# Half-array side tiles made whole, and the order of a chunked recurrence rebuilt, in a four-layer streaming encoder

## The chip, the cores and the metric

The kernel runs on one core of one Trainium2 chip. The metric is device time in microseconds (us). Before the change three runs gave a median of 2739.07 us (2736.65 to 2741.68). Engines are named as in the profile: PE (TensorE matmul), PEld (its weight load), DVE (VectorE), ACT (ScalarE), POOL (GpSimd), SP (SyncE, which issues the DMAs).

## The reference, cut to what matters

320 columns are processed at once: 256 frames of a prompt and 64 frames of a running stream ("sample") that has a cache of 512 frames. The model width is 2048. Every layer is `x + W_out(mixer(rmsnorm(x)) * silu(gate))`, and the mixers of the four layers are A, B, C, A:

```python
# A: differential attention, 16 heads of 2x64
p = attn_map(q1, k1) - lam * attn_map(q2, k2);  o = p @ v_all
o = o * rsqrt(mean(o * o) + 1e-5) * subln_g
# B: sparse attention, 16 heads of 128 on 4 key heads; an indexer picks the top keys
# C: RWKV-7, 32 heads with a 64x64 state, a scan over frames
sa = st @ (-kk_t)
st = st * w_t + outer(sa, kk_t * a_t) + outer(v_t, k_t)
o_t = st @ r_t
# then a group norm of o per head, a bonus term, and the gate
```

## The kernel before

**The main stream.** Every projection is a chain of 128-row weight tiles (`MTile`). A weight tile is loaded, split on ACT and DVE into a high and a low part in a `ring`, and multiplied in 16 k-steps of three fp32r matmuls of 320 columns; these are the rows with `ring` in their input. A `Group` of one tile runs its 16 k-steps in turn; a group of several tiles is "outer": for each quarter of the k-steps it goes through all its tiles, so it holds one PSUM bank for each tile from its start. `start_group` must have all of a group's banks before its first matmul. Banks 0 and 1 are kept for accumulators; banks 2 to 7 are shared with the side work, and an outer group may take any that is free.

**The side work.** Attention, norms, and the recurrence are Python generators (tasks of a `Stage`). A program-time planner (`Model`, `Sched.pump`) puts their instructions between the k-steps of the main stream. It gives out an operation of a task when its model says that the inputs are ready; for PE it adds `SLACK`, 400 ns, so that the main stream isn't held up. The order is fixed in the program; at run time each engine works its queue in order.

**Layer A** (twice, 16 heads each). `sample(h)` computes the sample's scores for both maps on 128 rows (64 frames of map 1, then of map 2), takes each map's exponential into its own 64-row buffer (`PS`), joins them with lambda, and transposes the joined map with five transposes whose input has 64 rows. `attend(h)` does the same for the prompt and then all of the head's value products: six matmul records on the whole array, and ten for the sample that write 64 rows each (four matmuls of `cv`, the two halves of the array in turn, and one of `vt` with 64 input rows). An fp32 matmul leaves two records, a transpose one. The end of the head transposes the output `ot` in three pieces, the third with 64 input rows.

**Layer B**: the sample's value product of each pair of heads ends in a matmul with 64 input rows; there are eight pairs.

**Layer C** runs stages v, then k and r, then g. In the k stage `on_k` (16 times) has a three-piece group of sums and a three-piece transpose, each with a 64-row third piece; `finish_rstd` (five times in the kernel) is built alike. `batch(n)` inverts 32x32 blocks of the recurrence in 31 steps of a multiply and a subtract, on POOL for the first two batches and on DVE for the last. The g stage (stage `sg`) runs 16 gate tiles, and beside them 16 chains, one for a pair of heads: `load_chain` takes a set of buffers (`SETS`: three at first, a fourth and a fifth later) and issues five loads; `corners` finishes the inverse with two bursts of small matmuls; `steps` walks over chunks 0 to 3 of the prompt, with three bursts of PE work for each chunk (products into `scr`, through ACT; products with `yv`, through ACT; the new state and the output), and a second task walks over the sample's chunk 4 with three more. Then `chain` loads the bonus (`bv_d`), norms and gates the output, transposes it in three pieces, marks the operand `opo` of the output projection, and gives its set back. The scratch bank of `corners`, the bank of `steps` and that of the last transpose are taken and given back apart.

**After layer C** the output projection begins with an outer group of four tiles; its first quarter needs the results of chains 0 to 3 only, its last quarter those of chains 12 to 15. **The end** of the kernel (`ending`) multiplies 16 result tiles by the norm, four pieces on DVE and two on POOL, and stores each.

Of the kernel before, what the change touches and what calls it, by code (L numbers as in the profile page):

```python
# [16 lines left out]
D = 2048  # L17
KT = 16
# [10 lines left out]
NEG = -1.0e30  # L29

# [73 lines left out]
class Model:  # L104
# [39 lines left out]
    def cost(self, op):  # L144
# [21 lines left out]
        if op.eng == "G":  # L166
# [8 lines left out]
            return 2.3 * n + 149  # L175
# [43 lines left out]
class Sched:  # L219
# [45 lines left out]
    def pump(self):  # L265

        while True:
            self.moved, nxt = False, None
            for t in list(self.tasks):
                while self.settle(t):  # L270
# [3 lines left out]
                    r = max(self.model.ready(op) + (SLACK if op.eng == "PE" else 0.0) for op in t.queue[:n])  # L274
# [111 lines left out]
class Stage:  # L386
    def __init__(self, prev):
        self.prev = prev
        self.active = 0
        self.closed = False  # L390
# [58 lines left out]
def hybrid_kernel(ctx: ExitStack, tc: tile.TileContext, a, o, layers=DEPTH):  # L449
# [71 lines left out]
    def transposes(dst, src, n=128):  # L521

        idn = ident[0:n, 0:n]
        PE.transpose(dst[:, 0:n], src[:, 0:128], idn)
        PE.transpose(dst[:, n:2 * n], src[:, 128:256], idn)
        PE.transpose(dst[0:64, 2 * n:3 * n], src[:, 256:320], idn)

    def copy_tokens(dst, src, n=128):
        S.copy(dst[:, 0:2 * n], src[:, 0:2 * n])
        S.copy(dst[0:64, 2 * n:3 * n], src[0:64, 2 * n:3 * n])  # L530
# [119 lines left out]
    def finish_rstd(li, sq):  # L650
# [3 lines left out]
        for b in range(3):  # L654
            n = 128 if b < 2 else 64
            for i, x in enumerate((ssum, sq)):
                PE.matmul(bk.ap[0:n, b:b + 1], lhsT=x[:, b * 128:b * 128 + n], rhs=ones[:, 0:1],
                          start=i == 0, stop=i == 1)
        G.memset(sm.ap[:, 0:3], 1.0)
        V.tensor_scalar(sm.ap[:, 0:2], bk.ap[:, 0:2], 1.0 / D, 1e-6, op0=OP.mult, op1=OP.add)  # L660
        V.tensor_scalar(sm.ap[0:64, 2:3], bk.ap[0:64, 2:3], 1.0 / D, 1e-6, op0=OP.mult, op1=OP.add)
# [5 lines left out]
        for b in range(3):  # L667
            n = 128 if b < 2 else 64
            PE.transpose(bk.ap[:, b * 128:b * 128 + n], rtok[0:n, b:b + 1].to_broadcast([n, 128]), ident[0:n, 0:n])
# [5 lines left out]
    def out_groups(li, opo, prev):  # L675
# [47 lines left out]
        return ([Group(mts[0:4], on_start=lambda: spawn(st, prefetch()))] + [Group([x]) for x in mts[4:]]  # L723
                + [close], st)

    def ending(sq, yall):
        yield from finish_rstd(layers, sq)
        yield from wait(*[("y", i) for i in range(KT)])
        for n, (k0, k1, E) in enumerate(((0, 3, V), (12, 14, G), (3, 6, V), (6, 9, V), (14, 16, G), (9, 12, V))):
            t = yall[:, k0:k1]  # L730
            E.tensor_mul(t, t, rstd.unsqueeze(1).to_broadcast([128, k1 - k0, T]))
# [8 lines left out]
    def layer_a(j, li, opn, opo, prev):  # L740
# [13 lines left out]
        PS = lay.slots(4, 576)  # L754
        PT = lay.slots(2, 384)
        PTS = lay.slots(2, T)
# [35 lines left out]
        def prep():  # L792
# [4 lines left out]
            for p in PP.free:  # L797
                G.memset(p[0:64, 64:128], 0.0)
                G.memset(p[0:64, 320:384], 0.0)
            if li:  # L800
# [94 lines left out]
        def sample(h):  # L895
# [31 lines left out]
            yield  # L927

            V.reciprocal(s[0:64, 4:6], s[0:64, 2:4])
            V.scalar_tensor_tensor(s[0:64, 6:7], s[0:64, 2:3], lam[0:64], s[0:64, 5:6], op0=OP.mult, op1=OP.mult)  # L930
            V.scalar_tensor_tensor(p1.ap[0:64], p2.ap[0:64], s[0:64, 6:7], p1.ap[0:64], op0=OP.mult, op1=OP.add)
            p2.rel()
            bk = yield from banks.one()
            for i in range(4):
                PE.transpose(bk.ap[:, i * 64:(i + 1) * 64], p1.ap[0:64, 64 + i * 128:192 + i * 128],
                             ident[0:64, 0:64])
            PE.transpose(bk.ap[0:64, 256:320], p1.ap[0:64, 0:64], ident[0:64, 0:64])
            p1.rel()
# [1471 lines left out]
```

## Time and profile before

| | |
|---|---|
| runs before, median of 3 | 2739.07 us |
| the profiled execution's own time | 2740.95 us |
| its span, first to last instruction | 2739.1 us |
| PE busy | 2677.7 us |
| DVE busy | 1926.6 us |
| ACT busy | 1466.7 us |
| POOL busy | 437.3 us |
| mean granted TensorE clock | 0.990 |

The span is the time from the first to the last instruction of the profiled execution; what lies outside it is the difference to its own time. Busy times are sums for each engine; engines overlap.

### The profile page before, as it was taken

The page shows a single profiled execution, that of the slowest core. Times are in us where ns is not written, and L with a number is a line of the kernel's source. Part 1 is how long each engine was busy: PE and PEld are TensorE (multiplying, and loading weights), DVE is VectorE, ACT ScalarE, POOL GpSimd, SP SyncE. Part 2 cuts the span into 40 slices and gives each one's busy share as a digit, 9 for nine tenths or more (in the row PEclk, how much of TensorE's full clock was granted, in tenths as well). Part 3 has the DMA queues.
Part 4 walks back from the last instruction along what each step waited for, and adds up shares of the span by engine and source line. Part 5 has one row for each costly group of instructions (what it writes and reads, how often), then busy time and mean ns, then how long its engine had stood idle before and what let it go on. Part 6 is the DMA issues. An engine that isn't in the chain of part 4 may idle for free.

```text
span 2739.1 us, 53165 instructions
## 1 busy us (share of the span) xinstructions
PE 2677.7 (98%) x19594; PEld 2569.3 (94%) x19594; DVE 1926.6 (70%) x4080; ACT 1466.7 (54%) x3582; POOL 437.3 (16%) x809
## 2 busy tenths in 40 slices
PE   8999999999999999989999999999899999999997
PEld 7999999999999999989999998888799999999997
DVE  7777777765898766459766767766657777777654
ACT  5666656554444444436644453566544666666553
POOL 2000000011000000122012745365310000000011
PEclk9999999999999999989999999999999999999998
DMA  6444444455334333665667676766464444444452
GB/s 227 149 152 155 153 149 149 145 180 178 133 130 150 122 134 135 201 173 173 224 181 207 184 201 176 243 222 205 129 199 165 151 154 154 153 145 153 133 176 105
DMA packets 219979, 455.23 MB, mean 166 GB/s; under 512 B 83270, under 2 KB 149254, under 8 KB 185798
## 3 DMA queue, kind: packets, MB, share of 16 engines
q1 hardware_dynamic: 219718, 451.83, 50.6%
q8 instruction: 154, 2.52, 0.4%
q14 instruction: 107, 0.88, 0.1%
HBM read 394.20 MB, written 57.55 MB: 165 GB/s over the span
## 4 chain that ended last, share of the span: by engine, by line
PE 51%; DVE 2%; DMA 1%; issue 1%; SPq 0%; POOL 0%; ACT 0%; DVEq 0%; POOLq 0%; ACTq 0%
PE psum L209 51%; DVE arena L209 1%; SPq L209 0%; DMA rec_d<-arena 0%; DVE ring L209 0%; DMA arena<-l_d 0%; DMA raw<-in_c_w_rkvg_dram 0%; DVE op_b L209 0%; POOL arena L209 0%; ACT ring L209 0%; POOL smt L209 0%; DVEq L2406 0%; DVE op_a L209 0%; ACT arena L209 0%; DVE smt L209 0%
## 5 line engine op out<-in xcount | busy, mean ns | idle before, releaser
L209 PE MATMUL psum<-op_a,ring 128*128 128x320 f32 x8496 | 1332.4, 314 | 22.4 <-ACT op_a L209 12.4
L209 PEld LDWEIGHTS psum<-op_a,ring 128*128 128x128 f32 x8496 | 1260.2, 189 | 38.8 <-ACT op_a L209 14.5
L209 ACT CAST ring<-raw 128x512 fp32r<-128x512 f32 (+2 forms) x1228 | 754.0, 618 | 846.8 <-PE psum L209 789.1
L209 DVE TENSOR_TENSOR ring<-raw,ring 128x512 fp32r<-128x512 f32 (+2 forms) x1228 | 852.2, 699 | 443.1 <-ACT ring L209 425.9
L209 PE MATMUL psum<-op_b,ring 128*128 128x320 f32 (+1 forms) x6240 | 990.9, 314 | 5.3 <-ACT ring L209 5.3
L209 PEld LDWEIGHTS psum<-op_b,ring 128*128 128x128 f32 (+1 forms) x6240 | 921.7, 188 | 21.2 <-ACT ring L209 5.6
L209 DVE TENSOR_TENSOR arena<-psum,arena 32x320 f32<-32x320 f32 (+3 forms) x567 | 269.9, 476 | 79.8 <-PE psum L209 60.1
L209 PE MATMUL psum<-arena 128*64 128x64 f32 (+9 forms) x3428 | 297.8, 253 | 3.3 <-DVE arena L209 2.2
L209 PEld LDWEIGHTS psum<-arena 128*64 128x64 f32 (+4 forms) x3428 | 238.7, 147 | 51.4 <-issue 23.0
L209 ACT COPY arena<-psum 128x256 f32<-128x256 f32 (+9 forms) x473 | 145.2, 331 | 95.4 <-PE psum L209 82.1
L209 ACT ACTIVATE arena<-psum,smt 64x128 f32<-64x128 f32 (+5 forms) x384 | 169.6, 442 | 25.5 <-DVE smt L209 15.8
L209 POOL TENSOR_TENSOR smt<-smt,mhalf 128x3 f32<-128x3 f32 (+1 forms) x64 | 74.9, 1170 | 476.2 <-DVE smt L209 466.2
L209 POOL TENSOR_TENSOR arena<-arena 128x64 f32<-128x64 f32 (+18 forms) x218 | 135.3, 624 | 38.8 <-DMA arena<-l_d 9.7
L209 PE MATMUL psum<-cst,arena 128*128 128x128 f32 (+3 forms) x807 | 130.5, 266 | 7.6 <-DVE arena L209 6.0
L209 PEld LDWEIGHTS psum<-cst,arena 128*128 128x128 f32 (+3 forms) x807 | 92.3, 134 | 30.6 <-issue 18.6
L209 POOL MEMSET smt<- 128x3 f32 (+2 forms) x85 | 8.4, 100 | 703.9 <-DVE smt L209 703.9
L209 ACT ACTIVATE arena<-arena 128x320 f32<-128x320 f32 (+1 forms) x192 | 89.1, 472 | 42.9 <-DVE arena L209 28.8
L209 POOL TENSOR_TENSOR ssum<-ssum,arena 128x320 f32<-128x320 f32 x70 | 64.3, 919 | 298.4 <-ACT arena L209 295.1
L209 ACT CAST op_b<-arena 128x320 fp32r<-128x320 f32 (+4 forms) x198 | 78.8, 416 | 53.4 <-DVE arena L209 30.0
L209 DVE TENSOR_TENSOR arena<-arena 64x320 f32<-64x320 f32 (+13 forms) x243 | 100.0, 420 | 3.4 <-DMA arena<-l_d 0.6
L209 ACT CAST op_a<-arena 128x320 fp32r<-128x320 f32 (+2 forms) x136 | 59.9, 442 | 66.3 <-DVE arena L209 47.5
L209 DVE TENSOR_TENSOR op_b<-arena,op_b 128x320 fp32r<-128x320 f32 (+4 forms) x198 | 85.9, 455 | 1.8 <-ACT op_b L209 1.6
(95 smaller groups left out, 1370.5 us busy)
## 6 DMA issues: line engine op xcount, KB each, us to landing
raw<-in_a_w_in_dram SPq DMA_DIRECT2D x120, 1024.0 KB, 5.2
raw<-in_c_w_rkvg_dram SPq DMA_DIRECT2D x52, 1024.0 KB, 5.7
raw<-in_w_out_dram SPq DMA_DIRECT2D x48, 1024.0 KB, 5.1
raw<-in_b_w_in_dram SPq DMA_DIRECT2D x45, 1024.0 KB, 4.9
raw<-in_w_out_dram SPq DMA_DIRECT2D x64, 256.0 KB, 3.8
arena<-rec_d SPq DMA_DIRECT2D x16, 962.5 KB, 5.5
raw<-in_c_w_rkvg_dram SPq DMA_DIRECT2D x48, 256.0 KB, 4.1
out_dram<-arena SPq DMA_DIRECT2D x72, 160.0 KB, 5.1
```

The source lines that it names most:

```text
L209: return getattr(self.engines[op.eng], op.name)(*op.args, **op.kw)
```

## The change

Five groups of edits:

1. **Whole tiles.** The third piece of every three-piece group is the frames 192 to 319 instead of 256 to 319 (`BLOCKS`), so that it has 128 rows like the others. In layer A the two exponentials of the sample become one on 128 rows, five transposes of 128x128 go back into the bank of the scores, the value product becomes five matmuls of the whole array with both maps on its output rows, and lambda and the sums are applied after it. In layer B the last piece is filled up with zeros.
2. **The recurrence.** `corners`, `steps` and `chain` become one task; the sample's chunk 4 goes in step with chunk 0; one bank is held from the corners to the last transpose. The set is given back at the last step; what follows (`gated`) uses a buffer apart (`ES`, one at first, two more once the last batch is inverted). There are four sets from the start.
3. **Orders.** The slack of stage `sg` is 0. The last batch of inverses runs on POOL. `rb` in `on_k` is spread by ACT and not by POOL.
4. The output projection after layer C begins with an outer group of six tiles.
5. `ending` multiplies on DVE alone, in five pieces.

```diff
+BLOCKS = (0, 128, 192)
...
-            return 2.3 * n + 149
+            return (3.3 if 64 < op.width < 128 else 2.3) * n + 149
...
-                    r = max(self.model.ready(op) + (SLACK if op.eng == "PE" else 0.0) for op in t.queue[:n])
+                    slack = SLACK if t.stage is None else t.stage.slack
+                    r = max(self.model.ready(op) + (slack if op.eng == "PE" else 0.0) for op in t.queue[:n])
...
-        for b in range(3):
-            n = 128 if b < 2 else 64
-            PE.transpose(bk.ap[:, b * 128:b * 128 + n], rtok[0:n, b:b + 1].to_broadcast([n, 128]), ident[0:n, 0:n])
+        for b, t in enumerate(BLOCKS):
+            PE.transpose(bk.ap[:, t:t + 128], rtok[:, b:b + 1].to_broadcast([128, 128]), ident)
...
-        return ([Group(mts[0:4], on_start=lambda: spawn(st, prefetch()))] + [Group([x]) for x in mts[4:]]
+        return ([Group(mts[0:(6 if li == 2 else 4)], on_start=lambda: spawn(st, prefetch()))] + [Group([x]) for x in mts[(6 if li == 2 else 4):]]
...
-        for n, (k0, k1, E) in enumerate(((0, 3, V), (12, 14, G), (3, 6, V), (6, 9, V), (14, 16, G), (9, 12, V))):
+        for k0, k1 in ((0, 4), (4, 8), (8, 11), (11, 14), (14, 16)):
...
-            p1, p2 = yield from PS.get(2)
-            for e, p in enumerate((p1, p2)):
-                S.activation(p.ap[0:64].rearrange("p (b c) -> p b c", c=288), in_banks(sc.ap[HALF[e]]), AF.Exp,
-                             bias=s[HALF[e], 1:2], scale=0.125, accum_out=s[0:64, 2 + e:3 + e])
+            p, = yield from PS.get(1)
+            S.activation(p.ap[:, 64:640].rearrange("p (b c) -> p b c", c=288), in_banks(sc.ap), AF.Exp,
+                         bias=s[:, 1:2], scale=0.125, accum_out=s[:, 2:3])
+            yield
+            for i in range(5):
+                PE.transpose(sc.ap[:, i * 128:(i + 1) * 128], p.ap[:, i * 128:(i + 1) * 128], ident)
...
-            for i in range(4):
-                PE.matmul(ob.ap[HALF[i % 2], 256:384], lhsT=pts.ap[:, i * 64:(i + 1) * 64],
-                          rhs=cv.ap[:, i * 128:(i + 1) * 128], start=i < 2, stop=i == 3)
-            PE.matmul(ob.ap[0:64, 256:384], lhsT=pts.ap[0:64, 256:320], rhs=vt.ap[0:64, 256:384],
-                      start=False, stop=True)
+            for i in range(5):
+                PE.matmul(ob.ap[:, 256:384], lhsT=pts.ap[:, i * 128:(i + 1) * 128],
+                          rhs=cv.ap[:, i * 128 - 128:i * 128] if i else vt.ap[:, 256:384], start=i == 0, stop=i == 4)
...
-            PE.transpose(bk.ap[:, 256:320], ot.ap[0:64, 256:384], ident[0:64, 0:64])
+            PE.transpose(bk.ap[:, 256:384], ot.ap[:, 256:384], ident)
...
-            PE.matmul(ob.ap[:, 0:128], lhsT=vt.ap[0:64, 256:384], rhs=pt.ap[0:64, 512:640], start=False, stop=True)
+            PE.matmul(ob.ap[:, 0:128], lhsT=vt.ap[:, 256:384], rhs=pt.ap[:, 512:640], start=False, stop=True)
...
-        sb, sl, sg = Stage(sv), Stage(sv), Stage(sk)
+        sb, sl, sg = Stage(sv), Stage(sv), Stage(sk, 0.0)
...
-                G.tensor_copy(rb.ap.rearrange("p (b f) -> p b f", f=64),
-                              sm.ap[:, 8:14].unsqueeze(2).to_broadcast([128, 6, 64]))
+                S.copy(rb.ap.rearrange("p (b f) -> p b f", f=64),
+                       sm.ap[:, 8:14].unsqueeze(2).to_broadcast([128, 6, 64]))
...
-            E = V if n == len(batches) - 1 else G
+            E = G
...
-        SETS = Slots(sched, sets[0:3])
+        SETS = Slots(sched, sets)
+
+        late = [(lg.ap(384), lg.ap(T)) for _ in range(2)]
+        ES = Slots(sched, [(cst[:, 128:512], rstd)])
...
+        def load_bonus(p):
+            yield from wait(("late", p))
+            e = yield from ES.get()
+            Q.dma_start(e.ap[1], bv_d[p])
+            flags["es", p] = e
...
+        def chain(ps):
+
+            yield from corners(ps)
+            for p in ps:
+                spawn(sg, load_bonus(p))
+            for c in range(4):
+                now = [Step(p, c, 0) for p in ps]
+                if not c:
+                    now += [Step(p, 4, 1) for p in ps]
+                for x in now:
+                    for e in range(2):
+                        PE.matmul(x.scr[HALF[e]], lhsT=x.mv[:, 0, e, x.c], rhs=x.st[:, e, x.c, :],
+                                  start=True, stop=True)
+                if c == 3:
+                    for p in ps:
+                        flags["late", p] = True
...
+            for p in ps:
+                got = flags["load", p]
+                Q.dma_start(o["new_c_wkv"][p], fields(got.ap)[5])
+                got.rel()
+                spawn(sg, gated(p))
...
+        def gated(p):
+            bank = flags["bank", p]
             bo = bank.ap
...
+            yield from wait(("es", p))
+            es = flags["es", p]
+            (ot, rh), sq = es.ap, bo[:, 0:384]
...
+            for b in range(3):
+                PE.transpose(bo[:, 128 * b:128 * b + 128], ot[:, 128 * b:128 * b + 128], ident)
...
             def chains():
-                for p in range(KT):
-                    yield from load_chain(p)
-                    spawn(sg, corners(p))
-                    spawn(sg, chain(p))
+                for p in range(0, KT, 1):
+                    ps = range(p, p + 1)
+                    for x in ps:
+                        yield from load_chain(x)
+                    spawn(sg, chain(ps))
```

## Rows read from the trace of the kernel before

**Rows 1.** The page, busy time and share of the span by engine

```profile
PE 2677.7 (98%) x19594; PEld 2569.3 (94%) x19594; DVE 1926.6 (70%) x4080; ACT 1466.7 (54%) x3582; POOL 437.3 (16%) x809
```

**Rows 2.** Windows of 60 us: stretch, length, busy us (instructions) by engine, clock, DMA

```profile
1920.00:1980.00 60.00, 52.54 (x479) 43.89 (x480) 37.32 (x84) 29.07 (x95) 24.40 (x42) 0.89 0.35 107
1980.00:2040.00 60.00, 60.00 (x411) 60.00 (x410) 36.04 (x54) 29.73 (x54) 9.01 (x10) 1.00 0.61 202
```

**Rows 3.** Timeline of PE in a head of layer A: start, busy us, what

```profile
314.65 1.93 PE L209 MATMUL psum<-op_a,ring 128*128 128x320 f32 x12
316.42 0.58 PE L209 MATMUL psum<-cst,arena 128*128 128x128 f32 x3
316.93 2.03 PE L209 MATMUL psum<-op_a,ring 128*128 128x320 f32 x12
318.88 0.51 PE L209 MATMUL psum<-cst,arena 64*128 64x64 f32 x5
319.33 4.23 PE L209 MATMUL psum<-op_a,ring 128*128 128x320 f32 x27
323.39 0.27 PE L209 MATMUL psum<-cst,arena 128*128 128x128 f32 x1
...
323.95 0.38 PE L209 MATMUL psum<-cst,arena 128*128 128x128 f32 x2
324.08 2.00 PE L209 MATMUL psum<-op_a,ring 128*128 128x320 f32 x12
325.92 1.77 PE L209 MATMUL psum<-arena 128*128 128x128 f32 x16
327.63 5.54 PE L209 MATMUL psum<-op_a,ring 128*128 128x320 f32 x36
```

**Rows 4.** Timeline of PE in layer B, at a sample's value product

```profile
970.76 1.12 PE L209 MATMUL psum<-op_a,ring 128*128 128x320 f32 x6
971.72 2.33 PE L209 MATMUL psum<-arena 128*128 128x128 f32 x16
973.80 20.04 PE L209 MATMUL psum<-op_a,ring 128*128 128x320 f32 x135
```

**Rows 5.** PE groups by form, window 1733 to 1957: the ring's records

```profile
L209 PE MATMUL psum<-op_b,ring 128*128 128x320 f32 x530 | 103.5, 328 | 0.0
...
L209 PE MATMUL psum<-op_a,ring 128*128 128x320 f32 x133 | 26.2, 328 | 0.0
```

**Rows 6.** Timeline of PE among the chains of layer C

```profile
1905.63 1.14 PE L209 MATMUL psum<-op_b,ring 128*128 128x320 f32 x6
1906.71 0.56 PE L209 MATMUL psum<-arena 64*64 64x64 f32 x12
1907.20 0.71 PE L209 MATMUL psum<-op_b,ring 128*128 128x320 f32 x3
1907.84 0.33 PE L209 MATMUL psum<-arena 64*64 64x64 f32 x4
1908.10 1.15 PE L209 MATMUL psum<-op_b,ring 128*128 128x320 f32 x6
```

**Rows 7.** Timeline of PE at the end of layer C, idle time in brackets

```profile
1959.79 0.34 PE L209 MATMUL psum<-arena 128*64 128x64 f32 x4
1960.46 0.33 PE L209 MATMUL psum<-arena 64*64 64x64 f32 x4 [0.34 <-ACT arena L209]
...
1972.15 1.16 PE L209 MATMUL psum<-op_a,ring 128*128 128x320 f32 x2 [1.79 <-ACT op_a L209]
```

**Rows 8.** Timeline of SP: a chain's bonus load, and the next chain's load

```profile
1827.67 0.33 SPq L209 DMA_DIRECT2D arena<-bv_d  x1
...
1840.87 0.32 SPq L209 DMA_DIRECT2D arena<-rec_d  x1
```

**Rows 9.** The chain of waits at the kernel's end: start, us, what

```profile
2727.12 1.16 DVE arena L209
...
2730.68 3.47 DVE arena L209 x2
```

More of the change, by code (lines that the diff above doesn't have):

```diff
@@ L386, with __init__ @@
 class Stage:
[L387 to L388 removed]
+    def __init__(self, prev, slack=SLACK):
+        self.prev, self.slack = prev, slack
         self.active = 0
@@ L653, in finish_rstd @@
         sm = yield from SM.get()
-        for b in range(3):
-            n = 128 if b < 2 else 64
+        for b, t in enumerate(BLOCKS):
             for i, x in enumerate((ssum, sq)):
[L657 to L661, printed above, removed]
+                PE.matmul(bk.ap[:, b:b + 1], lhsT=x[:, t:t + 128], rhs=ones[:, 0:1], start=i == 0, stop=i == 1)
+        V.tensor_scalar(sm.ap[:, 0:3], bk.ap[:, 0:3], 1.0 / D, 1e-6, op0=OP.mult, op1=OP.add)
         bk.rel()
@@ L666, in finish_rstd @@
         bk = yield from banks.one()
-        for b in range(3):
-            n = 128 if b < 2 else 64
-            PE.transpose(bk.ap[:, b * 128:b * 128 + n], rtok[0:n, b:b + 1].to_broadcast([n, 128]), ident[0:n, 0:n])
+        for b, t in enumerate(BLOCKS):
+            PE.transpose(bk.ap[:, t:t + 128], rtok[:, b:b + 1].to_broadcast([128, 128]), ident)
         V.tensor_copy(rstd, bk.ap[:, 0:T])
@@ L799, in prep @@
                 G.memset(p[0:64, 320:384], 0.0)
+            for p in PS.free:
+                G.memset(p[:, 0:64], 0.0)
+            for p in OT.free:
+                G.memset(p[64:128, 256:384], 0.0)
             if li:
@@ L1717, in gen @@
                 bk = yield from banks.one()
[L1718 to L1721 removed]
+                for b, x in enumerate(BLOCKS):
+                    PE.matmul(bk.ap[:, 2 * b:2 * b + 2], lhsT=sq.ap[:, x:x + 128], rhs=blk2, start=True, stop=True)
                 sq.rel()
                 sm = yield from SM.get()
[L1724 to L1726 removed]
+                V.tensor_scalar(sm.ap[:, 0:6], bk.ap[:, 0:6], 1e-24, None, op0=OP.max)
                 bk.rel()
@@ L1738, in gen @@
                 bk = yield from banks.one()
-                for b in range(3):
-                    n = 128 if b < 2 else 64
-                    PE.transpose(bk.ap[:, b * 128:b * 128 + n], rb.ap[0:n, b * 128:b * 128 + 128], ident[0:n, 0:n])
+                for b, x in enumerate(BLOCKS):
+                    PE.transpose(bk.ap[:, x:x + 128], rb.ap[:, b * 128:b * 128 + 128], ident)
                 rb.rel()
@@ new lines, in layer_c, with __init__ @@
+        class Step:
+            def __init__(self, p, c, sample):
+                self.c, self.sample = c, sample
+                cm, cs, y, kt, self.pc, zf, self.zb = fields(flags["load", p].ap)
+                bo = flags["bank", p].ap
+                self.rh = c5(y, 160)[:, :, 96:160]
+                self.mv = cm.rearrange("p (e s c x) -> p s e c x", s=2, e=2, x=64)
+                self.st = cs.rearrange("p (e c v) -> p e c v", e=2, v=64)
+                self.ktv, self.yv = c5(kt, 128), c5(y, 160)[:, :, 0:64]
+                self.z = zf[:, 64 * sample:64 * sample + 64]
+                self.zero = not sample and c == 0
+                self.here = [self.st[HALF[e], e, c] for e in range(2)]
+                self.scr = bo[:, 384 + 64 * sample:448 + 64 * sample]
+                self.dst = bo[64 * (c % 2):64 * (c % 2) + 64, (c // 2) * 128:(c // 2) * 128 + 128]
```

240 lines of the change are left out of this document (94 added, 146 removed).

## The prediction

> **What bounds the kernel now.** First the page's busy times: PE works 98% of the span and the next engine, DVE, 70% [rows 1]. So the question for every edit is what it takes from PE's queue or from PE's idle time. Then the windows: in a plain projection stage PE starts 411 matmuls in 60 us, 0.146 us each [rows 2]; a row of 135 ring matmuls gives 0.1465 [rows 4], the price used below. Where a stretch lasts longer than its ring matmuls at that price, the rest is side work, idle time or a lower clock. The third view, the timeline of PE, gives each burst of side work its price: the time between two starts, less the ring matmuls between them. The idle time is small, some 61 us in the whole span, and the windows show one piece of it that this change touches: at the end of layer C PE is busy 52.5 of 60 us and the granted clock falls to 0.89, between full speed and the half (1.2 GHz) [rows 2].
>
> **The price of a half tile.** In [rows 6] the three ring matmuls between two bursts of 64x64 tiles, 1907.20 to 1907.84, take 0.64 us where three cost 0.44. Leaving one tile shape and entering another thus costs 0.20 us a burst beyond the burst's own products. A whole 128x128 transpose costs the difference of a row of one and a row of two, 0.38 - 0.27 = 0.11 us [rows 3], and has no such charge; a whole matmul record of 128 columns I take at the same 0.11.
>
> **Side tiles, term by term.**
> - Five transposes of the sample: 316.93 to 319.33 is 2.40, less 12 ring matmuls 1.76, leaves 0.64 us [rows 3]. Five whole ones: 0.55. Gain 0.09.
> - The value product: 324.08 to 327.63 is 3.55, less 12, leaves 1.79 for 16 records [rows 3]. Sixteen whole ones: 1.76. Gain 0.03. The columns streamed become more and the charges go.
> - The transposes of `ot`: 314.65 to 316.93 is 2.28, less 12, leaves 0.52 [rows 3]; as the half tile's exit (half of the 0.20) falls after the last of these starts, 0.62. Three whole ones: 0.33. Gain 0.29.
> - A head thus gives 0.41; 32 heads 13.1 us.
> - Layer B: 970.76 to 973.80 is 3.04, less 6, leaves 2.16 for 16 records, 14 whole and 2 of 64 rows [rows 4]. Sixteen whole: 1.76. Gain 0.40, eight times: 3.2.
> - The same three-piece transpose stands 16 times in `on_k`, 16 times at a chain's end and five times in `finish_rstd`: 37 x 0.29 = 10.7. The other three-piece groups, of sums, I cost at nothing: fewer charges, more columns.
>
> Sum: 27 us. These stretches hold no idle time of PE, so the gain shows in full if nothing else is late. Added on other engines: a copy of 640 columns on ACT for two smaller ones, against an exponential and two DVE operations saved; the spread of `rb` goes to ACT, which is busy 54%. All of it lies under the main stream.
>
> The Trainium skill, "TensorEngine Tiling (Array Packing)", Key Properties, says that a change of tiling mode drains TensorE; by that rule, the trace agrees: 0.20 us a burst. The same page's Theoretical Speedup speaks against the change: a product with a dimension of at most 64 may go twice as fast on half tiles. By the first rule the sum above stands; by the second alone the whole tiles would cost time, and that is rival 5.
>
> **The recurrence.** Between 1733 and 1957, 224 us with no idle time of PE before the ring's rows, there are 663 ring matmuls [rows 5], 97.1 us; the other 126.9 are the chains' work, 7.9 for each of 16. The change leaves its products as they are. It removes bursts: a chain has 17 phases of PE work now (two of corners, three for each of five chunks) and 14 after, since the sample's three go with chunk 0. What a phase saves when it joins another: a lone burst of four records costs 1907.20 to 1908.10, less 3 ring matmuls, 0.46; one of twelve costs 1905.63 to 1907.20, less 6, 0.69; so four more cost 0.115, and joining saves 0.345 [rows 6]. If all 48 removed phases stood alone now, 16.6 us; if all already share a burst with another chain, nothing. The chains overlap now (the burst of twelve is such a meeting), so I take 6.
>
> The slack of 0 brings each phase 0.4 us earlier. Its price is that PE may reach a phase before ACT or DVE has ended; behind it waits the whole main stream. The trace of before shows such a wait only where there was no filler: 0.34 us [rows 7]. Upper bound: 224 phases (16 x 14) x 0.34 = 76; lower bound: nothing, as no idle time stood there with the slack. The planner still goes by its own ready times, and I take 3 us.
>
> **The end of layer C.** The last full run of side work begins at 1959.79, and the main stream runs on at 1972.15 [rows 7]: 12.4 us that hold some 2.3 us of work, then about 16 slow matmuls, 2 us: some 12 us lost. What is late there is the last chain. Its set came late: a chain asks for its bonus at 1827.67, and the next chain's load follows at 1840.87, 13 us of norm and gate during which the set only waits [rows 8]; this repeats through all 16 chains. With the set given back at the last step these 13 us leave a cycle of some 60 (16 chains from 1733 to 1972, 15 us each, on four sets), and each phase is 0.4 us earlier, so the last chain ends before the gate tiles do. Six tiles instead of four also lengthen the three quarters that don't need the last chains: two tiles x 12 k-steps x 3 x 0.1465 = 10.5 us of filler. Each alone covers most of the loss. Against it: an outer group of six needs six banks at once, two of its own and four of the shared six, and every chain holds one from corners to gate. I take a gain of 10 (bounds 0 and 12).
>
> The last batch of inverses moves from DVE to POOL, which was busy 24 of 60 us at the stage's end [rows 2]; chain 12, the first that needs it, comes three buffer rounds later. That is its cover; without it, the two late `ES` buffers would come late and the first chains would hold their banks longer. The loads are the same five for a chain, four sets' in a row where three and then a fourth went before; the six-tile group adds six smaller weight loads to SP. All at nothing: the weights are loaded three buffers ahead.
>
> **The kernel's end.** DVE multiplies three tiles in 1.16 us alone, 0.39 each; its four pieces end at 2730.68 + 3.47 = 2734.15, 7.03 after the start, as it is held up while POOL works [rows 9]. Sixteen tiles alone: 16 x 0.39 = 6.2. Gain 0.8, say 1; both bounds near it.
>
> **Sum.** -27 - 6 + 3 - 10 - 1 = -41 us. Against the profiled execution's 2740.95: 2700. The median of the runs shown lies 1.9 lower, so I predict 2698.
>
> **Rivals.**
> 1. *The banks of the six-tile group.* Chains still hold more than two shared banks when the gate tiles end; the group can't start and PE has only chain phases. For: the group takes four of six. Against: by the set's shorter cycle at most two chains are left then. The gain of 10 is gone: 2708 and up to 2716 if the wait adds to it. Chance 0.17.
> 2. *The early phases wait.* Each of 224 phases waits 0.1 us on average: 22 instead of 3, so 2717. For: the wait in [rows 7]. Against: planned times have held so far with room. Chance 0.12.
> 3. *Slower: the waits decide.* The same mechanism at 0.2 us a phase costs 45 and eats all of the gain; from 0.2 us on the kernel is slower, and at 0.34 it gives 2771. Place: PE's idle time before the chains' rows. Chance 0.05.
> 4. *Denser chains.* All removed phases stood alone, and four chains meet more often: 16 instead of 6, the tail whole: 2686 and less. Chance 0.11.
> 5. *Half tiles are cheap.* The streamed columns decide and the charge isn't spared. A half-size transpose or record then costs 0.055 against 0.11: 5 x 0.055 + 10 x 0.055 + 0.055 = 0.88 more a head, 28 us in layer A and 2 in the 37 other transposes; with the recurrence's terms 2741 + 30 - 14 = 2757. Against it: the ten half records cost as much now as ten whole ones [rows 3]. Chance 0.03. The Trainium skill's speedup rule, named above, would bring the time to this rival's.
> 6. *The edits don't shorten the path*, because weights or DVE set the pace as soon as PE is quicker; within 0.2% of 2739. Against: DVE at 70% [rows 1]. Chance 0.03.
>
> The forecast itself, 2687 to 2707, has 0.49. The range reaches into rivals 1, 2 and 4: 2680 to 2720. A measurement of this kernel can tell about 0.2%, 5.5 us, from no change. Faster 0.90 (the forecast, rivals 1, 2, 4 and an edge of 3), same 0.03, slower 0.07.
>
> **What would show it.** In a head of layer A no PE row of 64 rows or columns among transposes of the sample, of `ot`, or the value product, and 0.41 us less side work; a head of four weight tiles that much shorter. In the g stage fewer bursts between ring rows and less than 121 us of chain work; no PE idle time there. At the end of layer C ring rows without a gap and a clock of 1.00. DVE's last pieces end 6.2 us after `rstd`. The prediction is wrong if idle time of PE appears before 64-column rows (rivals 2, 3), if the gap at the start of the output projection stays (rival 1), or if heads of layer A don't get shorter (rivals 5, 6).

## The result, and the profile after

The changed kernel takes 2711.88 us (median of 4 runs, 2707.03 to 2713.39), the kernel before beside it 2737.86 us (4 runs, 2736.14 to 2741.68): a ratio of 0.990, interval 0.9883 to 0.9918. The profiled execution took 2710.41 us, against 2740.95 before: 30.5 us went by the two profiles and 26.0 by the medians, where 41 were forecast.

PE's row on the page shows the same number of matmuls as before [rows 1] and 28 us less busy time:

```profile
PE 2649.7 (98%) x19594; PEld 2577.8 (95%) x19594; DVE 1879.7 (69%) x3966; ACT 1442.7 (53%) x3466; POOL 438.4 (16%) x808
```

To see where the time came from, both traces are cut at the same main-stream matmuls: a stage lasts from the start of its first ring matmul to that of the next stage's first. The ring matmuls are the same in both kernels and stand in the same order.

| stage | before | after | gain | forecast |
|---|---|---|---|---|
| layer A, both | 1099.64 | 1095.19 | 4.45 | 13.1 |
| layer B | 420.39 | 417.04 | 3.35 | 3.2 |
| layer C, k and r | 328.20 | 321.37 | 6.83 | 4.6 (`on_k`) |
| layer C, g, and the output projection behind it | 376.42 | 361.22 | 15.20 | 17.6 (4.6 + 6 + 10 - 3) |
| last output projection and end | 130.69 | 129.57 | 1.12 | 1 |

The other stages differ by 0.3 us or less, some up and some down; the 1.4 us forecast for five `finish_rstd` lie among them and do not show. Two terms are far off: layer A gave a third of its sum, and the g stage has nearly its sum, but not from the parts that I named.

**Layer A.** PE's timeline in a head, as in [rows 3]:

```profile
313.07 1.05 PE L210 MATMUL psum<-op_a,ring 128*128 128x320 f32 x6
313.96 1.04 PE L210 MATMUL psum<-cst,arena 128*128 128x128 f32 x8
314.75 9.92 PE L210 MATMUL psum<-op_a,ring 128*128 128x320 f32 x66
324.81 0.33 PE L210 MATMUL psum<-cst,arena 128*128 128x128 f32 x1
324.90 0.69 PE L210 MATMUL psum<-op_a,ring 128*128 128x320 f32 x3
325.42 0.38 PE L210 MATMUL psum<-cst,arena 128*128 128x128 f32 x2
325.56 2.01 PE L210 MATMUL psum<-op_a,ring 128*128 128x320 f32 x12
327.40 1.95 PE L210 MATMUL psum<-arena 128*128 128x128 f32 x16
329.11 2.44 PE L210 MATMUL psum<-op_a,ring 128*128 128x320 f32 x15
```

Everything that the change makes is there. No row has 64 rows or columns, the transposes of the sample and of `ot` share one burst of eight, and 313.07 to 314.75 less six ring matmuls (0.88) leaves 0.80 us for it, where two bursts had 0.52 and 0.64 [rows 3]. The value product still leaves 1.79 in this head; counted with the ring matmul behind it, it takes 1.81 us before and 1.79 after in the mean. What is new is one small transpose, the first of three of the prompt's map: 314.75 to 324.90 is 10.15 us for 66 ring matmuls (9.67) and one transpose, so it costs 0.48 us. In [rows 3] the first of the three came out of the same place for 0.11. The same place one head earlier, in the timeline of the weight loads (PEld), where the wait shows in brackets, and the DVE timeline beside it:

```profile
291.06 0.14 PEld L210 LDWEIGHTS psum<-cst,arena 128*128 128x128 f32 x1 [0.40 <-DVE arena L210]
```

```profile
287.00 0.49 DVE L210 TENSOR_TENSOR op_b<-arena,op_b 128x320 fp32r<-128x320 f32 x1 [0.31 <-ACT op_b L210]
287.41 0.21 DVE L210 SCALAR_TENSOR_TENSOR smt<-smt,lamt 128x2 f32<-128x2 f32 x1
287.54 0.68 DVE L210 TENSOR_TENSOR ring<-raw,ring 128x512 fp32r<-128x512 f32 x1
288.14 2.48 DVE L210 TENSOR_TENSOR arena<-psum,arena 128x320 f32<-128x320 f32 x5
290.66 0.75 DVE L210 SCALAR_TENSOR_TENSOR arena<-arena,smt 128x128 f32<-128x128 f32 x2
```

The transpose reads what the last row writes, the joining of the map's two halves. It starts at 291.06, as soon as the first of the two joining operations is done (290.66 and half of 0.75). Ahead of the joining DVE works off, among others, the low half of a finished head (`op_b`, 0.49) and five rope operations (2.48). Before, the order was the other:

```profile
288.62 0.75 DVE L209 SCALAR_TENSOR_TENSOR arena<-arena,smt 128x128 f32<-128x128 f32 x2
289.28 0.49 DVE L209 TENSOR_TENSOR op_b<-arena,op_b 128x320 fp32r<-128x320 f32 x1
289.68 1.48 DVE L209 TENSOR_TENSOR arena<-psum,arena 128x320 f32<-128x320 f32 x3
```

So my theory for the missing 9 us is: whole tiles deliver their 0.40 us a head (nearly 0.38 at the eight transposes, 0.03 at the value product), and DVE's order takes 0.36 of it back (0.47 less 0.11 us for that transpose, means over the heads between 200 and 500 us). Over both layers this transpose stands by itself in 27 of the 32 heads and takes 0.44 us in the mean: 8.8 us more than at 0.11.

**Layer B** needs no theory. The value product of [rows 4] is 2.66 us less six ring matmuls, 1.78 where it was 2.16:

```profile
966.07 1.13 PE L210 MATMUL psum<-op_a,ring 128*128 128x320 f32 x6
967.03 1.95 PE L210 MATMUL psum<-arena 128*128 128x128 f32 x16
968.73 20.04 PE L210 MATMUL psum<-op_a,ring 128*128 128x320 f32 x135
```

**The end of layer C.** The stretch that had a clock of 0.89 and 7.5 us of idle PE [rows 2] is full, and what idle time there is has moved ahead of it:

```profile
1860.00:1920.00 60.00, 56.81 (x763) 46.38 (x760) 46.25 (x111) 43.58 (x166) 44.47 (x85) 1.00 0.52 157
1920.00:1980.00 60.00, 60.00 (x424) 58.65 (x421) 39.81 (x68) 29.43 (x61) 12.42 (x15) 1.00 0.63 201
```

PE's timeline there shows what it is:

```profile
1909.82 1.54 PE L210 MATMUL psum<-arena 128*64 128x64 f32 x26
1912.45 1.13 PE L210 MATMUL psum<-arena 128*64 128x64 f32 x18 [1.09 <-ACT arena L210]
1913.51 0.55 PE L210 MATMUL psum<-cst,arena 128*128 128x128 f32 x3
1913.98 0.94 PE L210 MATMUL psum<-arena 128*64 128x64 f32 x14
1915.22 0.33 PE L210 MATMUL psum<-arena 64*64 64x64 f32 x4 [0.30 <-ACT arena L210]
1916.44 0.90 PE L210 MATMUL psum<-arena 128*64 128x64 f32 x14 [0.89 <-ACT arena L210]
1917.65 0.33 PE L210 MATMUL psum<-arena 64*64 64x64 f32 x4 [0.30 <-ACT arena L210]
1918.58 0.79 PE L210 MATMUL psum<-arena 128*64 128x64 f32 x10 [0.60 <-ACT arena L210]
1919.30 0.55 PE L210 MATMUL psum<-cst,arena 128*128 128x128 f32 x3
1919.78 0.34 PE L210 MATMUL psum<-arena 128*64 128x64 f32 x4
1920.04 1.58 PE L210 MATMUL psum<-op_a,ring 128*128 128x320 f32 x9
...
1929.50 0.49 PE L210 MATMUL psum<-cst 128*128 128x128 f32 x3
...
1937.31 0.49 PE L210 MATMUL psum<-cst,arena 128*128 128x128 f32 x3
```

From 1909.82 to 1920.04 no ring matmul stands in the timeline: the gate tiles have ended and the six-tile group has not begun. PE has chain phases only and waits 1.09 + 0.30 + 0.89 + 0.30 + 0.60 = 3.2 us in five places. That is the mechanism of rival 1, at a third of the ten us that it was given. A chain ends with three transposes: four chains still have theirs ahead of them when the gate tiles end, at 1913.51, 1919.30, 1929.50 and 1937.31, and the group begins when two are left. The last ones stand 32 us earlier than the last of before (1969.38), but 28 us behind the end of the gate tiles; it is the ring matmuls of the six tiles that run beside them.

PE's waits from the g stage to the end of the projection, before (1670 to 1990 us) and after (1670 to 1935 us): time in total, times, the longest.

```profile
PE psum L209 <- ACT ring L209: 5.3, 1, 5.3
PE psum L209 <- DVE arena L209: 4.2, 3, 1.5
PE psum L209 <- ACT op_a L209: 3.6, 2, 1.8
PE psum L209 <- ACT arena L209: 1.0, 2, 0.6
```

```profile
PE psum L210 <- ACT arena L210: 3.2, 5, 1.1
PE psum L210 <- DMA arena<-yr_d: 2.5, 1, 2.5
PE psum L210 <- ACT ring L210: 0.3, 1, 0.3
PE psum L210 <- DVE ring L210: 0.2, 1, 0.2
```

Of before's 4.2 us for DVE, 1.2 lie ahead of the stage. In the stage waits go from 12.8 to 6.2 us, 6.6 less: 4.3 at the end (2.9 for DVE, 3.6 and 1.0 against 3.2) and 2.3 at the start, where 5.3 us for a late weight tile became 2.5 for a chain's load. The side work itself, taken burst by burst (from the last ring matmul ahead of a burst to the second behind it, less two at the ring's price, PE's waits taken out), goes from 134.6 to 128.6 us, 6.0 less. The rest of 15.2, some 2.6 us, lies in ring matmuls away from any burst, and 2.1 of it in the projection: in the kernel before they stand 0.25 to 0.43 us apart between 1966.94 and 1976.5, under a granted clock of 0.50 (1.2 GHz from 1962.9 to 1976.5, behind PE's first waits at the gap), and none does in the changed kernel.

### The profile page after: what moved, and what is told of

Read it like the earlier page. It is cut to its first block, busy times and chain, and to the rows that moved or that the text cites. A ratio compares the mean times of both kernels' runs of the same rounds, so it can differ in the third digit from the quotient of the medians.

```text
span 2708.4 us, 52837 instructions
## 1 busy us (share of the span) xinstructions
PE 2649.7 (98%) x19594; PEld 2577.8 (95%) x19594; DVE 1879.7 (69%) x3966; ACT 1442.7 (53%) x3466; POOL 438.4 (16%) x808
## 4 chain that ended last, share of the span: by engine, by line
PE 48%; DVE 3%; issue 1%; DMA 1%; ACT 1%; POOL 0%; SPq 0%; DVEq 0%; POOLq 0%; ACTq 0%
PE psum L210 48%; DVE arena L210 2%; DVE ring L210 1%; ACT arena L210 1%; DMA arena<-yr_d 0%; DMA arena<-l_d 0%; DVE op_b L210 0%; DMA rec_d<-arena 0%; ACT op_a L210 0%; ACT ring L210 0%; DMA v_d<-arena 0%; POOL arena L210 0%; DVE smt L210 0%; DVE op_a L210 0%; ACT op_b L210 0%
## 5 line engine op out<-in xcount | busy, mean ns | idle before, releaser
L210 DVE TENSOR_TENSOR arena<-psum,arena 32x320 f32<-32x320 f32 (+1 forms) x535 | 260.7, 487 | 71.1 <-PE psum L210 57.0
L210 PE MATMUL psum<-arena 128*64 128x64 f32 (+8 forms) x3428 | 299.4, 251 | 7.2 <-ACT arena L210 3.2
L210 PEld LDWEIGHTS psum<-arena 128*64 128x64 f32 (+4 forms) x3428 | 254.2, 153 | 44.2 <-issue 17.8
L210 ACT COPY arena<-psum 128x384 f32<-128x384 f32 (+7 forms) x355 | 138.2, 397 | 113.2 <-PE psum L210 107.4
L210 ACT ACTIVATE arena<-psum,smt 64x128 f32<-64x128 f32 (+5 forms) x384 | 157.8, 412 | 70.1 <-PE psum L210 49.6
L210 POOL TENSOR_TENSOR arena<-arena 128x64 f32<-128x64 f32 (+27 forms) x280 | 179.2, 647 | 45.4 <-DMA arena<-l_d 14.8
L210 PE MATMUL psum<-cst,arena 128*128 128x128 f32 (+1 forms) x780 | 121.7, 275 | 13.1 <-DVE arena L210 5.6
L210 PEld LDWEIGHTS psum<-cst,arena 128*128 128x128 f32 (+1 forms) x780 | 94.0, 137 | 25.4 <-DVE arena L210 9.9
L210 DVE TENSOR_REDUCE smt<-psum 128x1 f32<-128x192 f32 (+5 forms) x176 | 65.7, 417 | 28.1 <-PE psum L210 21.6
```

Of the source, the lines that this page charges most:

```text
L210: return getattr(self.engines[op.eng], op.name)(*op.args, **op.kw)
```

## The experiments

Each kernel stands alone on the changed one unless it says otherwise. Stage times are cut as above. How far a stage's time carries is seen where its code is untouched: the g stage with its projection gives 361.2, 359.5, 358.4 and 361.6 us in four profiles of the same code, layer A 1094.8 to 1095.6 in six.

**e1: more slack for layer A's side work.**

```diff
-        st = Stage(prev)
+        st = Stage(prev, 800.0)
```

> The changed kernel with the planner's slack of both layer A stages 800 ns instead of 400; nothing else. Theory: in layer A the whole tiles gave 0.4 us a head and a new wait took most of it back: the first transpose of the prompt's map reaches PE 0.3 us before DVE, whose queue has five rope operations ahead, has joined the maps. With 0.4 us more slack that wait goes: the two layer A stages take 1085 us together instead of 1095.2, the kernel 2701. Rival: whole tiles of 128 columns are dearer than I priced them; then the slack changes nothing, 1095 +- 1. Second rival: the wait only moves to the next operation that PE needs; 1092 to 1097.

Layer A 1097.8 us, kernel 2714.91 (2737.56 for the kernel before on the same chip). The theory's number fell; the result is a little above the second rival's range. A later place for PE's side work does not cure DVE's order. What the transpose loses falls to 0.27 us, but a new wait stands in PE's list (120 to 540 us), for the split of a weight tile on DVE:

```profile
PE psum L210 <- DVE ring L210: 3.1, 10, 0.3
```

**e2: the kernel before with the whole tiles of layers A and B alone.** From the changed kernel it takes `attend` of both layers, `transposes` and `copy_tokens`; the recurrence, the six tiles, the slack and the kernel's end stay as before.

```diff
-            PE.transpose(bk.ap[:, 256:320], ot.ap[0:64, 256:384], ident[0:64, 0:64])
+            PE.transpose(bk.ap[:, 256:384], ot.ap[:, 256:384], ident)
```

> The kernel before with the whole tiles of layers A and B alone (and the overlapping last block of the value transposes that they need); recurrence, slack, groups, norms and the end as before. Theory: the wait in layer A comes with these tiles themselves, so layer A gains 4 to 6 us in its two stages (1099.6 before) and layer B 3 (420.4 before): 2732 in all. Rival: the wait comes from other edits; then layer A gains its 13 us and the kernel is at 2723.

Layer A 1096.0, layer B 417.3, the g stage and projection 376.9, kernel 2729.44 us (2737.56 before). So the tiles of A and B give what they give in the whole change, and the loss in layer A comes with them: DVE has the same order, and the first transpose costs 0.48. In layer C the g stage gains nothing from them. The k and r stage, whose code is that of before, took 323.5 us here and 328.2 in the kernel before; how far that stage scatters is taken up below.

**e5: the low half of a finished head on POOL, out of DVE's way.**

```diff
-            V.tensor_sub(opo.lo(h), t.ap, opo.hi(h).bitcast(F32))
+            G.tensor_sub(opo.lo(h), t.ap, opo.hi(h).bitcast(F32))
```

> The changed kernel with one DVE operation a head of layer A, the low part of the head's result (0.49 us, ahead of the joining of the maps in DVE's queue), moved to POOL, which is idle there. Theory: in layer A PE waits because DVE's queue is full at that one place of a head; 0.5 us less in it takes the wait of 0.36 us a head away: the two layer A stages go from 1095.2 to 1084 to 1088 us. Rival: the operation on POOL slows DVE beside it as at the kernel's end, where DVE took 2.48 us for 1.16; then 1093 to 1098.

Layer A 1105.5, ten us slower than the changed kernel; kernel 2717.48 us (2741.96 before). The joining is now first in DVE's queue, as wanted, but runs beside POOL's subtraction. DVE, then POOL, then PE:

```profile
289.95 1.37 DVE L210 SCALAR_TENSOR_TENSOR arena<-arena,smt 128x128 f32<-128x128 f32 x2
```

```profile
290.01 1.02 POOL L210 TENSOR_TENSOR op_b<-arena,op_b 128x320 fp32r<-128x320 f32 x1 [23.39 <-ACT op_b L210]
```

```profile
291.46 0.41 PE L210 MATMUL psum<-cst,arena 128*128 128x128 f32 x2 [0.57 <-DVE arena L210]
```

Two joining operations take 1.37 us where they take 0.75 alone; they end at 291.32, 0.29 behind POOL's end at 291.03, and PE waits 0.57 us for them. The rival's mechanism is right; the loss is 7 us beyond its range. The Trainium skill, "SBUF — State Buffer", section "SBUF: two separate sides", says that DVE with two SBUF inputs and a GpSimd operation that reads SBUF lock each other out for a whole instruction. By that rule the second joining operation runs after POOL's; the trace agrees in that its record ends only 0.29 us behind POOL's end, but the first one's record (289.95 to 290.30) overlaps POOL's by 0.29 us.

**e9: the order alone.** The low half of a head waits until the next head's map is joined.

```diff
             p2.rel()
+            flags["joined", li, h] = True
...
             S.copy(opo.hi(h), t.ap)
+            if h < 15:
+                yield from wait(("joined", li, h + 1))
             yield
```

> The changed kernel with one order changed in layer A: the low part of a head's result is given to DVE only after the next head's maps are joined. DVE's queue then has the joining ahead of that operation and of the five rope operations, with no work added or taken away. Theory: the wait in layer A is an order in DVE's queue; with the joining first it goes, and the whole tiles' 0.4 us a head show: the two layer A stages take 1082 to 1088 us (1095.2 changed), the kernel 2700 to 2704. Rival: DVE is full at that place; then the wait moves to the weight split behind it, as with the larger slack, and the stages take 1093 to 1098.

Layer A 1089.2 us: 6.0 less than the changed kernel, 10.4 less than before, and 1 above the range expected. DVE's and PE's timeline:

```profile
285.69 0.75 DVE L210 SCALAR_TENSOR_TENSOR arena<-arena,smt 128x128 f32<-128x128 f32 x2
286.35 0.48 DVE L210 TENSOR_TENSOR op_b<-arena,op_b 128x320 fp32r<-128x320 f32 x1
```

```profile
283.72 2.80 PE L210 MATMUL psum<-op_a,ring 128*128 128x320 f32 x18
286.36 0.64 PE L210 MATMUL psum<-cst,arena 128*128 128x128 f32 x3
286.75 2.00 PE L210 MATMUL psum<-op_a,ring 128*128 128x320 f32 x12
```

The joining is first, and the three transposes share a burst; 283.72 to 286.75 is 3.03 us, less 18 ring matmuls 0.39. Counted with the ring matmul behind them they take 0.47 in the mean over the heads, where before's burst of one and burst of two took 0.33; so some 0.13 a head is still lost, 4.3 us in 32 heads. With it 10.4 + 4.3 = 14.7, beside my 13.1. Over four runs the kernel takes 2704.06 us (2703.89 to 2704.42) against 2739.58 (7 runs): 0.9875, interval 0.9858 to 0.9891. Its slowest run is faster than the changed kernel's fastest, though on another chip, and the intervals of the two ratios overlap a little.

**e3: the g stage with the old slack of 0.4 us.**

```diff
-        sb, sl, sg = Stage(sv), Stage(sv), Stage(sk, 0.0)
+        sb, sl, sg = Stage(sv), Stage(sv), Stage(sk)
```

> The changed kernel with the slack of the recurrence's stage back at 400 ns. Stages g and the output projection after it took 376.4 us before and 361.2 after. Theory: the slack of 0 costs PE no waits among the chains and only brings them forward, so with 400 the chains end later, the six-tile group waits longer for its banks, and the two stages take 363 to 368 us. Rival, as I predicted: a slack of 0 costs PE waits; then 358.

The stage and its projection take 368.4 us, some 8 more than the 360 of the changed kernel; kernel 2718.04 us (2737.56 before). That is the theory, at the upper end of its range. The waits that I priced for slack 0 appear with the slack, not without it, and the projection starts 5 us later (Cg, the part before it, 249.8 instead of 244.6):

```profile
PE psum L210 <- ACT arena L210: 7.5, 15, 1.7
```

**e12: slack 0 alone, on the kernel before.**

```diff
-        sb, sl, sg = Stage(sv), Stage(sv), Stage(sk)
+        sb, sl, sg = Stage(sv), Stage(sv), Stage(sk, 0.0)
```

> The kernel before with the slack of the recurrence's stage 0 and nothing else of the change. Theory, after the changed kernel lost 7 us with the slack back at 400: the slack only makes chains late; without it each chain of before ends some 6 us earlier and the 12 us lost at the end of layer C shrink: 368 to 373 us for the two stages. Rival, as predicted: PE waits for phases issued too early; 377 to 380.

377.1 us, no gain over 376.4; kernel 2739.33 us (2736.17 before). The rival's number holds, though not by phases issued too early. By itself the earlier place is worth nothing, and the last chain is as late as ever: PE has one wait of 4.9 us for it.

```profile
PE psum L209 <- DVE arena L209: 6.1, 2, 4.9
```

**e6: a chain's set given back at the end of norm and gate, as before.**

```diff
-                got.rel()
                 spawn(sg, gated(p))
...
             es.rel()
+            flags["load", p].rel()
```

> The changed kernel, but a chain gives its set of buffers back after its gate, as before the change, and not at its last step; all else as changed. Stages g and output projection after it: 361.2 us changed, 376.4 before. Theory: the early return is what lets the chains end before the main stream needs them; with 13 us more in a set's cycle the last chains end some 30 us later, the six-tile group waits for their banks, and the two stages take 370 to 380 us. Rival: chains are paced by PE's interleaving and the return matters little; 361 to 365.

385.0 us, 24 more than the changed kernel and 8 more than the kernel before, beyond the range expected; kernel 2734.09 us (2741.96 before). PE waits 10.0 us in 20 places for ACT, and the projection starts 19 us later (Cg 264.0 instead of 244.6). Without the early return the rest of what was changed in these two stages is a loss.

```profile
PE psum L210 <- ACT arena L210: 10.0, 20, 1.3
```

**e8: the sample's chunk as a step by itself, ahead of chunk 0.**

```diff
-            for c in range(4):
-                now = [Step(p, c, 0) for p in ps]
-                if not c:
-                    now += [Step(p, 4, 1) for p in ps]
+            for k in range(5):
+                c = max(k - 1, 0)
+                now = [Step(p, c, 0) if k else Step(p, 4, 1) for p in ps]
```

> The changed kernel with the sample's chunk 4 as a step of its own ahead of chunk 0 instead of in step with it: 17 phases of PE work a chain, one after the other, instead of 14. Theory: the lone bursts cost PE little, since chains meet each other anyway (the changed kernel's chains take PE 5.5 us less than before, 4.6 of it the whole transposes); but each chain becomes 5 us longer, so chains end later and the two stages take 365 to 372 us, by waits. Rival, as I predicted: 48 phases more cost PE 6 to 16 us of work and no waits.

375.4 us, 14 to 17 more; kernel 2724.06 us (2741.96 before). The side work, counted as above, is 137.5 instead of 128.6 us, 8.9 more for 48 phases, and PE waits 6.2 us for ACT in 14 places instead of 3.2 in five. So the theory was half right: the waits came, but the phases are not free, and their work lies in the rival's range.

**e4: a first group of four tiles behind layer C.**

```diff
-        return ([Group(mts[0:(6 if li == 2 else 4)], on_start=lambda: spawn(st, prefetch()))] + [Group([x]) for x in mts[(6 if li == 2 else 4):]]
+        return ([Group(mts[0:4], on_start=lambda: spawn(st, prefetch()))] + [Group([x]) for x in mts[4:]]
```

> The changed kernel with an outer group of four tiles instead of six at the start of the output projection after layer C. Theory: PE's main stream stands still from 1909.8 to 1920.0 because the group of six waits for banks that chains hold, with 3 us of idle time in it; four tiles find their banks, and the chains end early enough without the filler: 358 us for the two stages. Rival: the two tiles more of filler are what covers the last chains; then the gap of before comes back in part, 365 to 370 us.

364.3 us, 3 to 6 more; kernel 2714.32 us (2737.56 before). It falls between the two numbers, nearer to the rival's. The projection starts earlier (Cg 236.3 instead of 244.6), and the old gap is back in small, ring matmuls behind the last chain's gate:

```profile
1948.48 6.68 PE L210 MATMUL psum<-op_a,ring 128*128 128x320 f32 x32 [2.13 <-ACT op_a L210]
```

**e11: the group of six alone, on the kernel before.**

```diff
-        return ([Group(mts[0:4], on_start=lambda: spawn(st, prefetch()))] + [Group([x]) for x in mts[4:]]
+        n = 6 if li == 2 else 4
+        return ([Group(mts[0:n], on_start=lambda: spawn(st, prefetch()))] + [Group([x]) for x in mts[n:]]
```

> The kernel before with an outer group of six tiles after layer C and nothing else of the change. Stages g and output projection took 376.4 and 376.9 us in two profiles of the kernel before's recurrence. Prediction's step: 10.5 us more of filler covers most of the 12 us lost at the end of layer C by itself: 364 to 369. Rival: with chains as late as before's, the group waits for its banks instead, and the loss only moves ahead of it: 374 to 380.

373.3 us, 3 less than before and just under the rival's range; kernel 2735.81 us (2736.17 before). The gap at the end goes, and most of its loss comes back as a later start: Cg is 247.8 us instead of 226.8. With late chains the six banks come late.

**e7: the last batch of inverses on DVE, as before.**

```diff
-            E = G
+            E = V if n == len(batches) - 1 else G
```

> The changed kernel with the last batch of inverses on DVE as before. Theory: it is off the path on either engine: the two stages within 2 us of 361.2. Rival: DVE is then late for the weight split or the chains; 364 or more. Second rival: POOL was the brake on the first chains; 358 or less.

358.1 us for the g stage and its projection, 3 under the 361.2 that the theory allowed 2 us around, and at the edge of the second rival; but e5, with the batch on POOL, has 358.4. No difference between the engines shows beyond that spread. The whole kernel takes 2713.16 us (2741.96 before). Its k and r stage took 327.3 us where the nine other profiles of that code (the changed kernel and e1 to e10 without e2) have 321.4 to 322.9. The stretch from 1510 to 1560 us shows a granted clock of 0.93 here; but e9 has 0.93 at 1610 to 1660 and a stage of 321.6, so the cause is not settled.

**e10: e9 with a first group of five.**

```diff
-        return ([Group(mts[0:(6 if li == 2 else 4)], on_start=lambda: spawn(st, prefetch()))] + [Group([x]) for x in mts[(6 if li == 2 else 4):]]
+        return ([Group(mts[0:(5 if li == 2 else 4)], on_start=lambda: spawn(st, prefetch()))] + [Group([x]) for x in mts[(5 if li == 2 else 4):]]
```

> The same kernel with an outer group of five tiles after layer C instead of six. Stages g and output projection: 358 to 361 us with six in four profiles of the same code, 364 with four. Theory: the fifth tile's banks and the sixth's filler weigh about the same; 357 to 362. Rival: the wait for banks is what costs; 356 or less.

357.4 us for the stage and projection, 4 less than e9's 361.6 and a little below the lowest profile with six; one run took 2702.05 us. That is 0.07% under e9, less than the 0.2% that a measurement of this kernel can tell.

## Why the prediction was right, and where it was not

The time is inside the range, 14 us above the number, and the forecast's own range (to 2707) is missed by 5: of 41 us, 30.5 came. It lies in rival 1's range (2708 to 2716), but that is in part luck: rival 1's wait came at 3.2 us, and most of what is missing is layer A's. The g stage is near its sum only because errors of both signs met.

- **The price of half tiles held.** Layer B (3.35 for 3.2), the eight transposes in a head (0.38 in the mean, where 0.09 and 0.29 were forecast) and the value product (0.03, as forecast) are as worked out. With e9 layer A comes to 10.4 of the 13.1. Rival 5 fell: whole tiles with more streamed columns cost less. The Trainium skill, "TensorEngine Tiling (Array Packing)", Key Properties, says that a change of tiling mode drains TensorE; the trace agrees in layer B's product, 2.16 us with two records of 64 rows and 1.78 without. That page's Theoretical Speedup, up to twice, shows in none of the bursts that were made whole.
- **The step that failed first** is "These stretches hold no idle time of PE, so the gain shows in full if nothing else is late". Something was late: DVE's joining, which had started 0.66 us ahead of the low half (288.62, 289.28) and now starts 3.66 behind it (287.00, 290.66); what put it there is not shown. I read the idle time of PE, not how close DVE's result came before its reader. Rival 6 named DVE, but as a bound by its busy share; at 69% busy it was its order that counted. Shown by e2 (the loss comes with the tiles), e9 (the order alone gives 6 us back); e1 and e5 moved the wait or replaced it.
- **The recurrence, 6 for the merging, was mis-sized.** The side work of the two stages fell by 6.0, and 16 whole three-piece transposes at the forecast's price explain 4.6, so merging phases into one burst gave about 1. That separate chains met in bursts before, too, would explain it: the bursts are 124 before and 114 after, where 48 phases went. e8 does not fit this simply: the same 48 phases as a step by themselves cost 8.9, and why they cost more there is open.
- **Slack 0 had the wrong sign:** I charged 3 and e3 shows 8 gained in the changed kernel: with the old slack the chains end later and the projection starts 5 us later. Rivals 2 and 3 fell with it. Alone it gives nothing (e12).
- **The end of layer C** gave 6 to 7 of the 10: 7.5 us of waits went, rival 1's 3.2 came, and the clock gave back some 2. "So the last chain ends before the gate tiles do" is wrong: four chains were left there, not the two at most that rival 1 was weighed with, and the last ended 28 us later. The reason stands (e6: the early return decides), but "Each alone covers most of the loss" is wrong: six tiles alone give 3 (e11), slack alone nothing (e12), and with four tiles the other edits stay 3 to 6 us short (e4). The early return alone was not tried.
- **Not in my sum:** the 5.3 us wait for a weight tile ahead of the chains. In the trace of before the sync queue issued four stores of a chain's inputs over 11.03 us, from 1693.46, with weight loads behind them; after, three stores over 6.74 us. I had put weight loads at nothing. The wait stands at 4.7 to 5.8 us in e2, e11 and e12 and is gone in e3 to e8, so the tiles of layers A and B, the six tiles, the slack, the early return, the batch's engine and the sample's place are not it, each by itself; which edit moved these stores is open.
- **`on_k`, 4.6:** the two profiles differ by 6.8, but that is one pair. Profiles with the k and r code of before gave 323.5 to 328.2 us (before, e2, e11, e12), with that of after 321.4 to 322.9 (nine, e7 left out): 4 between their means, 3.6 with e7. PE's waits and clock make most of this scatter. The side work alone, counted as in the g stage, is 88.9 to 90.2 us in the four and 84.6 to 86.8 in all ten, 4.3 between the means, and the three transposes take 0.66 us before and 0.36 after where they stand by themselves, 0.30 for the forecast's 0.29. So the term is borne out.
- **The kernel's end** is right in mechanism and size. DVE's timeline, against [rows 9]: five pieces without POOL end 5.77 us after their start, and the stage is 1.1 shorter.

```profile
2696.85 5.77 DVE L210 TENSOR_TENSOR arena<-arena,rstd 128x1280 f32<-128x1280 f32 x5
```

## What to carry to other kernels

When PE's side work gets shorter, list for each burst the instruction that feeds it, and by how much its result came early; a reader with little to spare will wait if another engine's queue changes its order. An early return of a buffer, an earlier place and more filler are not three payments for one gap: here the earlier place was worth nothing alone and the filler 3 us, so a term for "any of them" is no sum. And a wait taken from the end may stand ahead of it, as here in front of the six banks: look for the next resource that the same late work holds.

## What the runs showed of the hardware

- A half piece among whole ones can cost more than a whole one: three transposes of `on_k`, the third with 64 input rows, took 0.66 us and three whole ones 0.36; five half transposes of the sample 0.64, five whole ones 0.55. Not every half shape does: the three transposes of `v` in layer A, the third of which wrote 64 rows before, take 0.33 us before and after, and the value product of layer A, ten of whose 16 records were half ones, went from 1.81 to 1.79. What decides is not shown. Whole records of 128 columns go by 0.11 us, however little of them is used (eight in a burst 0.88).
- DVE was slowed where it met POOL: 1.37 us for 0.75 in e5, and at the kernel's end 7.03 us for twelve tiles before, where it did 16 alone in 5.77 after.
- A stage's time can be steadier than its clock: in the stretch from 1610 to 1660 us the granted clock was 1.00 after and 0.93 in e9, with the same code, while the k and r stage took 321.4 and 321.6 us. PE also waits in that stretch, 7.3 and 6.8 us of 50.
